# Keeping VectorE's and ScalarE's instructions in source order in a decoder block on one Trainium2 core

## The chip, the core and the metric

The kernel runs on one core of a Trainium2 chip. TensorE (PE) multiplies matrices out of SBUF into banks of PSUM, VectorE (DVE) and ScalarE (ACT) work on tiles elementwise, GpSimd (POOL) does a few small things, and SyncE (SP) issues nearly all DMA transfers. Each engine works through its own list of instructions in order and waits at an instruction until what it needs is done. The metric is the device time of one launch in microseconds (us), as the median of several runs. The kernel before takes 1941.25 us.

## What is computed

One layer of a decoder trunk for 256 tokens of width 2048, all in float32: adaptive norms, two token mixers side by side (retention and a short gated convolution), merged by gates, then a gated feed-forward part with a depthwise convolution.

```python
mod = c_act @ w_ada[l] + b_ada[l]
sh1, sc1, g1, sh2, sc2, g2 = [m[:, None, :] for m in jnp.split(mod, 6, axis=-1)]
xn = _rmsnorm(h, norm1_g[l]) * (1.0 + sc1) + sh1
proj = xn @ w_in[l]
q, k, v, g_ret, bg, cg, xc, gate_logits = jnp.split(proj, splits, axis=-1)
...
y_ret = _retention_chunkwise(q, k, v).reshape(b, s, D_RET)
y_ret = (y_ret * jax.nn.silu(g_ret)) @ w_ret_o[l]
y_conv = bg * _causal_dwconv(cg * xc, w_sc[l])
y_conv = y_conv @ w_conv_o[l]
gates = jax.nn.sigmoid(gate_logits + b_gate[l])
gate_a, gate_b = jnp.split(gates, N_BRANCHES, axis=-1)
mixed = (gate_a * y_ret + gate_b * y_conv) @ w_mix_o[l]
h = h + g1 * mixed
xn2 = _rmsnorm(h, norm2_g[l]) * (1.0 + sc2) + sh2
up = xn2 @ w_up[l]
gt = _causal_dwconv(xn2 @ w_gate[l], w_ffconv[l], b_ffconv[l])
ff = (jax.nn.silu(gt) * up) @ w_down[l]
h = h + g2 * ff
return _rmsnorm(h, final_g)
```

## The kernel before

Nearly all time is matrix products with weights that are read once. A float32 product is made of float32r products: every weight tile is split into a rounded part `hi` (a cast on ACT, line 304) and the rest `lo` (a subtraction on DVE, line 305), and activations are kept split in the same way (`split`, lines 90 to 95).

The program is a list of **units**. A `Weights` unit loads a tile of 256 x 512 weights (`raw`, 512 KB, seven buffers), splits it and multiplies it: 16 matmuls in a block of `w_block` (weights stationary, four accumulators; 8 with `hi`, lines 409, and 8 half as wide with `lo`, line 414), 12 in a block of `x_block` (activations stationary, lines 376 to 378). Eight units make one block over the 2048 rows. When a block ends, ACT copies half of each accumulator (`sb`, line 420) and DVE adds the other half to it. An `Ada` unit loads a tile of `w_ada` into the same `raw` buffers and has no matmul: DVE alone adds it to an accumulator (`ada`, line 341). `spread` puts the `Ada` units between the `Weights` units. `Call` and `Loaded` units do single steps, such as a gate's bias and sigmoid, or a part of the second norm (`normed`).

The blocks follow each other so: a first stage in chunks (to about 390 us); the projections for retention with its rotations, scores and mixing (`rot_block`, `retention`), and three blocks C, X and B of the convolution's group 0; the retention's output projection; the convolution's groups 1 to 3 (`conv_blocks`: at the end of X the product u x cg, four scalings on ACT at line 746, and eight tap operations on DVE); the convolution's output projection, the mixing projection, the second norm (about 1195 us), and the feed-forward part.

The loop that writes the program takes a step per unit: it calls `load` for the unit nine places ahead, `prep` (the `hi` and `lo`, or the `ada`) for the unit two places ahead, `run` (the matmuls and what ends a block), and then the functions that earlier steps left for this one (`after`). That is the order of the source. It isn't the order on the engines: a scheduler orders each engine's instructions by data and buffers, and takes one ahead of another where it expects it to be ready, except where an instruction is told to keep its place (`tc.keep_in_program_order`, used in the first stage for a few).

Of the kernel before, what the change touches and what calls it, by code (L numbers as in the profile page):

```python
# [15 lines left out]
ALU = mybir.AluOpType  # L16
# [30 lines left out]
def tile_trunk_block(  # L47
# [6 lines left out]
    nc = tc.nc  # L54
    x, positions, out = x[0], positions, out[0]
# [34 lines left out]
    def split(src, dst):  # L90

        nc.scalar.copy(dst[:, :, 0, :], src)  # L92
        nc.vector.tensor_tensor(
            dst[:, :, 1, :], src, dst[:, :, 0, :].bitcast(F32), op=ALU.subtract
        )
# [10 lines left out]
    nc.vector.memset(warm, 0.0)  # L106
    nc.scalar.activation(warm, warm, AF.Sigmoid)
# [11 lines left out]
    def turned(vec, n, dst):  # L119
        pt = misc_bank()  # L120
        nc.tensor.transpose(pt[:, :n], vec[:n, :], ident[:n, :n])
        nc.vector.tensor_copy(dst, pt[:, :n])
        return dst
# [3 lines left out]
    nc.scalar.activation(c_act, c_raw, AF.Sigmoid)  # L127
    nc.vector.tensor_mul(c_act, c_act, c_raw)
# [96 lines left out]
    def sumsq(src, acc_col):  # L225
        junk = small.tile([P, 512], BF16, tag="junk", bufs=1, name=nm("junk"))
        n = src.shape[-1]
        return nc.scalar.activation(junk[:, :n], src, AF.Square, accum_out=acc_col)
# [5 lines left out]
    for t in range(2):  # L234
# [3 lines left out]
        nc.vector.tensor_reduce(ss_t, ss_x[:, t], axis=mybir.AxisListType.X, op=ALU.add)  # L238
        r_x = rstd_of(ss_t, 1, D, "r_x")
        nc.vector.tensor_scalar_mul(diag[t], ident, r_x[:, 0:1])  # L240
    x_t = [blk8("x_t", [P, 8, S], F32) for _ in range(2)]
    for g in range(8):
# [8 lines left out]
        nc.scalar.copy(x_t[g // 4][:, 2 * (g % 4):2 * (g % 4) + 2, :].rearrange("p k s -> p (k s)"), pt)  # L251
# [30 lines left out]
    class Weights:  # L282
# [11 lines left out]
        def prep(self):  # L294
# [9 lines left out]
            nc.scalar.copy(self.hi, self.raw)  # L304
            nc.vector.tensor_tensor(self.lo, self.raw, self.hi.bitcast(F32), op=ALU.subtract)  # L305
# [4 lines left out]
    class Ada:  # L310
# [23 lines left out]
        def prep(self):  # L334
            acc = self.state["acc"]
            for k in range(self.nk):
                kt = self.k0 + k
                if kt == 0 and not self.bias:
                    nc.vector.tensor_scalar_mul(acc, self.raw[:, k], c_act[:, 0:1])
                    continue  # L340
                nc.vector.scalar_tensor_tensor(  # L341
# [19 lines left out]
    def shift_of(ps, b, bias, k0, n):  # L361
        nc.vector.tensor_tensor(b[:, k0:k0 + n], ps, bias[:, k0:k0 + n], op=ALU.add)

    def scale_of(ps, a, bias, norm, k0, n):
        sl = slice(k0, k0 + n)
        nc.vector.tensor_tensor(a[:, sl], ps, bias[:, sl], op=ALU.add)
        nc.vector.scalar_tensor_tensor(
# [29 lines left out]
    def w_block(w, c0, xt, epilogue):  # L397
# [3 lines left out]
        def run_at(k0):  # L401
            def run(u):
                if k0 == 0:
                    st["ps"] = [acc_bank() for _ in range(4)]
                for i in range(4):
# [12 lines left out]
                    if last:  # L418
                        b = small.tile([P, S], F32, tag="sb", name=nm("sb"))
                        nc.scalar.copy(b, ps[:, S:2 * S])  # L420
# [14 lines left out]
    def xn1_ready(k0, k1):  # L435
        def done(acc):
# [4 lines left out]
            for k in sorted({k0, *range(k0 + k0 % 2, k1, 2)}):  # L441
                m = 1 if k % 2 else min(2, k1 - k)
                xk = x_t[k // 8][:, k % 8:k % 8 + m, :]
                for i in range(m):
                    kt = k + i
                    nc.scalar.activation(
# [18 lines left out]
    def start_block(j, in_psum):  # L465
# [8 lines left out]
        def finish(t, ps, n):  # L474
            d = dst[t]
            if in_psum or n == 0:
                nc.scalar.copy(d, ps)
            else:
                nc.vector.tensor_tensor(d, ps, d, op=ALU.add)
# [3 lines left out]
        def swish(d):  # L483
            sig = work.tile([P, CB], F32, tag="xtmp", bufs=2, name=nm("sig"))
            nc.scalar.activation(sig, d, AF.Sigmoid)
            nc.vector.tensor_tensor(d, d, sig, op=ALU.mult)
# [51 lines left out]
    def broadcast(acc, store, half, name, bank):  # L538
        if "t" not in store:
            store["t"] = blk8(name, [P, D], F32)  # L540
        for s in range(2):
# [3 lines left out]
            nc.scalar.copy(store["t"][:, c0:c0 + CB], ps)  # L545
# [43 lines left out]
    def rotate(xx, store, key):  # L589
        o = {}  # L590

        def turn(n):
            v = nc.vector.tensor_tensor
# [18 lines left out]
    def rot_block(col, store, key):  # L612
        xs = {}

        def e(i, a, b):
            if i == 0:
                xs["x"] = w4("qk", [P, 4, S])
            nc.vector.tensor_tensor(xs["x"][:, i, :], a, b, op=ALU.add)
# [4 lines left out]
    def retention(pair, st):  # L623

        def scores():
            st["pt"] = []
            pts = w4("pt", [P, 2, S + P])
            for h2 in range(2):
# [9 lines left out]
                nc.vector.tensor_tensor(pt[:, 0:S], ps[:, 0:S], st["dec"][:, h2, :], op=ALU.mult)  # L638
                nc.vector.tensor_tensor(pt[:, S:S + P], ps[:, S:S + P], st["dec"][:, h2, 0:P], op=ALU.mult)
# [3 lines left out]
        def mix():  # L643
# [78 lines left out]
    def conv_blocks(j):  # L722
        st = {}

        def e_c(i, a, b):
            if i == 0:
                st["c"] = w4("cg", [P, 4, S])
            nc.vector.tensor_tensor(st["c"][:, i, :], a, b, op=ALU.add)

        def e_x(i, a, b):  # L730
# [3 lines left out]
            nc.vector.tensor_tensor(st["u"][:, i, 2:S + 2], a, b, op=ALU.add)  # L734
# [5 lines left out]
        def gate_x():  # L740
            u = st["u"][:, :, 2:S + 2]
            st["y"] = w4("conv", [P, 4, S])
            nc.vector.tensor_tensor(u, u, st["c"], op=ALU.mult)
            for i in range(4):
                t = 4 * j + i
                nc.scalar.mul(st["y"][:, i, :], u[:, i, :], wsc[:, 32 + t:33 + t])

        def taps(i0):
            for i in range(i0, i0 + 2):
                u, y, t = st["u"][:, i, :], st["y"][:, i, :], 4 * j + i  # L750
                nc.vector.scalar_tensor_tensor(
                    y, u[:, 1:S + 1], wsc[:, 16 + t:17 + t], y, op0=ALU.mult, op1=ALU.add)
                nc.vector.scalar_tensor_tensor(
                    y, u[:, 0:S], wsc[:, t:t + 1], y, op0=ALU.mult, op1=ALU.add)

        def e_b(i, a, b):
            if i == 0:
                st["b"] = w4("bg", [P, 4, S])
            nc.vector.tensor_tensor(st["b"][:, i, :], a, b, op=ALU.add)
            if i == 3:  # L760
                after(1, lambda: nc.vector.tensor_tensor(st["y"], st["y"], st["b"], op=ALU.mult))
# [44 lines left out]
    def conv_o_block(j):  # L806
        cols = slice(j * CB, (j + 1) * CB)

        def e(t, ps):
            a, b = gate_a[t][:, cols], gate_b[t][:, cols]  # L810
            nc.vector.tensor_tensor(b, ps, b, op=ALU.mult)
            nc.vector.tensor_tensor(a, a, b, op=ALU.add)
# [26 lines left out]
    def residual(j, t, ps, gate):  # L839
        cols = slice(j * CB, (j + 1) * CB)  # L840
        tmp = work.tile([P, CB], F32, tag="xtmp", bufs=2, name=nm("res"))
        nc.vector.tensor_tensor(tmp, ps, gate["t"][:, cols], op=ALU.mult)
        nc.vector.tensor_tensor(h_tok[t][:, cols], h_tok[t][:, cols], tmp, op=ALU.add)
# [3 lines left out]
    def turn_h(j):  # L847
# [3 lines left out]
        for g in range(2):  # L851
# [7 lines left out]
            nc.scalar.copy(h_t[j // 2][:, k0:k0 + 2, :].rearrange("p k s -> p (k s)"), ps)  # L859
# [21 lines left out]
    def norm2():  # L881
        ss = small.tile([P, 2], F32, tag="ss2", name="ss_h2")
        nc.vector.tensor_reduce(ss, ss_h, axis=mybir.AxisListType.X, op=ALU.add)
        r = rstd_of(ss, 2, D, "r_h")
        dr = w4("dr", [P, 2, P])
        for t in range(2):
            nc.vector.tensor_scalar_mul(dr[:, t, :], ident, r[:, t:t + 1])
# [5 lines left out]
    def normed(k0, k1):  # L893
        for kt in range(k0, k1):
# [195 lines left out]
```

## Time and profile before

| | |
|---|---|
| time, median of 3 runs | 1941.25 us (1940.28 to 1943.81) |
| time of the profiled execution | 1944.93 us |
| its span | 1943.1 us |
| PE busy | 1876.3 us, 97% |
| DVE busy | 1380.0 us, 71% |
| ACT busy | 891.1 us, 46% |
| mean bandwidth of DMA | 233 GB/s |

The span is what the profile sees of one execution; 1.83 us of its time lie around it. An engine's busy time counts its instructions, not its waits. PE's clock is granted by the chip and shown as a share of full speed.

### The profile page before, as it was taken

How to read it: one execution, taken by the hardware profiler on the slowest of the kernel's cores; microseconds unless marked ns; L12 is line 12 of the kernel's file. 1: busy time of each engine (PE TensorE's matmuls, PEld its weight loads, DVE VectorE, ACT ScalarE, POOL GpSimd, SP SyncE). 2: the span in 40 equal slices, each digit the busy share in tenths (PEclk: the TensorE clock that was granted, in tenths of full speed). 3: DMA queues.
4: the chain of work that ended last, by engine and by line, in shares of the span. 5: the costliest groups of instructions: out<-in, count | busy, mean ns of one | idle time of the engine just before them, and what ended most of it. 6: DMA issues, size and time to landing. Idle time of an engine off the chain costs nothing.

```text
span 1943.1 us, 25273 instructions
## 1 busy us (share of the span) xinstructions
PE 1876.3 (97%) x9543; PEld 1582.6 (81%) x9543; DVE 1380.0 (71%) x1638; ACT 891.1 (46%) x1150; POOL 21.8 (1%) x51
## 2 busy tenths in 40 slices
PE   5999999999999999999989999999999999999997
PEld 4788888878888877888778777888888888888886
DVE  6899987867688865677677766777765556666655
ACT  4643444534334543444444445555554335555543
POOL 1000000000000000000000000000000000000000
PEclk9999999999999999999999999999999999999999
DMA  8889986667777777787777885777665556666553
GB/s 300 305 278 308 319 306 188 207 220 242 235 234 246 237 250 245 263 269 248 249 241 259 290 266 153 232 230 225 218 205 194 192 192 192 188 192 207 193 193 112
DMA packets 222091, 452.89 MB, mean 233 GB/s; under 512 B 14932, under 2 KB 27536, under 8 KB 221584
## 3 DMA queue, kind: packets, MB, share of 16 engines
q1 hardware_dynamic: 220768, 448.99, 70.3%
q10 hardware_dynamic: 720, 2.10, 0.3%
q8 instruction: 75, 1.23, 0.2%
q14 instruction: 48, 0.39, 0.1%
q0 software_dynamic: 480, 0.18, 0.0%
HBM read 449.11 MB, written 2.10 MB: 232 GB/s over the span
## 4 chain that ended last, share of the span: by engine, by line
PE 81%; DMA 9%; DVE 6%; issue 3%; ACT 1%; SPq 0%; POOL 0%; DVEq 0%; POOLq 0%; ACTq 0%
PE acc L409 30%; PE acc L414 15%; PE acc L377 12%; PE acc L378 12%; PE acc L376 12%; DMA raw<-in_w_ada 7%; DVE lo L305 3%; DVE ada L341 1%; DMA ld<-in_b_gate 1%; PE misc L355 1%; PE misc L247 0%; ACT hi L304 0%; DMA raw<-in_w_mix_o 0%; DMA raw<-in_w_in 0%; DVE y_tok L660 0%
## 5 line engine op out<-in xcount | busy, mean ns | idle before, releaser
L304 ACT CAST hi<-raw 128x1024 fp32r<-128x1024 f32 (+1 forms) x601 | 622.9, 1038 | 837.1 <-PE acc L409 426.5
L305 DVE TENSOR_TENSOR lo<-raw,hi 128x1024 fp32r<-128x1024 f32 (+1 forms) x601 | 717.9, 1203 | 302.4 <-ACT hi L304 299.3
L409 PE MATMUL acc<-xn,hi 128*128 128x512 f32 x2688 | 852.0, 398 | 5.6 <-DVE u L734 2.5
L414 PEld LDWEIGHTS acc<-xn,lo 128*128 128x128 f32 x2688 | 507.1, 189 | 129.6 <-DVE lo L305 9.9
L414 PE MATMUL acc<-xn,lo 128*128 128x256 f32 x2688 | 531.3, 279 | 6.7 <-DVE lo L305 6.7
L409 PEld LDWEIGHTS acc<-xn,hi 128*128 128x128 f32 x2688 | 412.9, 190 | 8.8 <-DVE u L734 2.9
L341 DVE SCALAR_TENSOR_TENSOR ada<-raw,c_act,ada 128x1024 f32<-128x1024 f32 (+2 forms) x199 | 238.9, 1201 | 177.6 <-DMA raw<-in_w_ada 176.9
L377 PE MATMUL acc<-lo,ff_t 128*128 128x512 f32 x332 | 129.2, 389 | 0.0
L376 PE MATMUL acc<-hi,ff_t 128*128 128x512 f32 x332 | 129.2, 389 | 0.0
L378 PE MATMUL acc<-hi,ff_t 128*128 128x512 f32 x332 | 129.2, 389 | 0.0
L376 PE MATMUL acc<-hi,xn 128*128 128x512 f32 x304 | 119.0, 395 | 4.1 <-ACT xn L92 2.4
L377 PE MATMUL acc<-lo,xn 128*128 128x512 f32 x304 | 119.8, 394 | 1.1 <-DVE lo L305 1.1
L378 PE MATMUL acc<-hi,xn 128*128 128x512 f32 x304 | 119.4, 393 | 0.0
L420 ACT COPY sb<-acc 128x256 f32<-128x256 f32 x168 | 61.9, 370 | 44.4 <-PE acc L414 28.4
L378 PE MATMUL acc<-hw,xn 128*128 128x512 f32 x208 | 82.0, 394 | 0.0
L377 PE MATMUL acc<-lw,xn 128*128 128x512 f32 x208 | 81.9, 394 | 0.0
L376 PE MATMUL acc<-hw,xn 128*128 128x512 f32 x208 | 81.1, 394 | 0.0
L304 ACT CAST hw<-raw 128x1024 fp32r<-128x1024 f32 (+1 forms) x58 | 55.6, 959 | 48.4 <-DMA raw<-in_w_in 27.2
L377 PEld LDWEIGHTS acc<-lo,ff_t 128*128 128x128 f32 x332 | 62.3, 188 | 13.2 <-DVE lo L305 0.2
L376 PEld LDWEIGHTS acc<-hi,ff_t 128*128 128x128 f32 x332 | 62.3, 188 | 13.0
L378 PEld LDWEIGHTS acc<-hi,ff_t 128*128 128x128 f32 x332 | 62.3, 188 | 12.7
L376 PEld LDWEIGHTS acc<-hi,xn 128*128 128x128 f32 x304 | 57.1, 188 | 17.7 <-ACT xn L92 2.4
(195 smaller groups left out, 1762.4 us busy)
## 6 DMA issues: line engine op xcount, KB each, us to landing
raw<-in_w_in SPq DMA_DIRECT2D x272, 512.0 KB, 4.7
raw<-in_w_ada SPq DMA_DIRECT2D x160, 512.0 KB, 4.6
raw<-in_w_gate SPq DMA_DIRECT2D x88, 512.0 KB, 4.1
raw<-in_w_up SPq DMA_DIRECT2D x88, 512.0 KB, 4.1
raw<-in_w_down SPq DMA_DIRECT2D x88, 512.0 KB, 4.3
raw<-in_w_ret_o SPq DMA_DIRECT2D x32, 512.0 KB, 5.2
raw<-in_w_conv_o SPq DMA_DIRECT2D x32, 512.0 KB, 5.0
raw<-in_w_mix_o SPq DMA_DIRECT2D x32, 512.0 KB, 6.1
```

The source lines that it names most:

```text
L304: nc.scalar.copy(self.hi, self.raw)
L305: nc.vector.tensor_tensor(self.lo, self.raw, self.hi.bitcast(F32), op=ALU.subtract)
L341: nc.vector.scalar_tensor_tensor(acc, self.raw[:, k], c_act[:, kt:kt + 1], acc, op0=ALU.mult, op1=ALU.add)
L355: nc.tensor.matmul(ps[:, i:i + 1], lhsT=flat[:, (s0 + i) * P:(s0 + i + 1) * P], rhs=ones[:, 0:1], start=True, stop=True,)
L376: nc.tensor.matmul(ps, lhsT=xh, rhs=u.hi[:, k, :], start=k0 + k == first, stop=False)
L377: nc.tensor.matmul(ps, lhsT=xh, rhs=u.lo[:, k, :], start=False, stop=False)
L378: nc.tensor.matmul(ps, lhsT=xl, rhs=u.hi[:, k, :], start=False, stop=k0 + k == end - 1)
L409: nc.tensor.matmul(ps, lhsT=u.hi[:, k, i * P:(i + 1) * P], rhs=xt(k0 + k).rearrange("p h s -> p (h s)"), start=k0 + k == 0, stop=False,)
L414: nc.tensor.matmul(ps[:, 0:S], lhsT=u.lo[:, k, i * P:(i + 1) * P], rhs=xt(k0 + k)[:, 0, :], start=False, stop=last and k == UK - 1,)
L420: nc.scalar.copy(b, ps[:, S:2 * S])
```

## The change

A small class stands in front of `nc.vector` and `nc.scalar`. Once `ordered[0]` is set, each instruction that is issued through it is told to keep its place in the order of the source among the instructions told so on its engine. It is set in the main loop from the unit `n_start` on, twelve units before the end of the first stage. All instructions of DVE and ACT from there on are ordered so; those of PE, SP and POOL stay with the scheduler. No instruction, tile or buffer is added or taken away.

```diff
+    ordered = [False]
+
+    class Ordered:
...
+        def __init__(self, engine):
+            self.engine = engine
+
+        def __getattr__(self, name):
+            fn = getattr(self.engine, name)
+
+            def issue(*args, **kw):
+                ins = fn(*args, **kw)
+                return tc.keep_in_program_order(ins) if ordered[0] else ins
+            return issue
+
+    vector, scalar = Ordered(nc.vector), Ordered(nc.scalar)
...
-            nc.scalar.copy(self.hi, self.raw)
-            nc.vector.tensor_tensor(self.lo, self.raw, self.hi.bitcast(F32), op=ALU.subtract)
+            scalar.copy(self.hi, self.raw)
+            vector.tensor_tensor(self.lo, self.raw, self.hi.bitcast(F32), op=ALU.subtract)
...
         now[0] = i
+        ordered[0] = i >= n_start
         units[i].run()
```

All other lines of the diff put `vector` and `scalar` where `nc.vector` and `nc.scalar` stood. In the lists below, line 67 is the line of `ins = fn(...)` in the new class, and stands for all of them.

DVE at the end of block X of the convolution's group 2, before (901 to 912 us). `u` is the accumulator's sum, `lo_` and `ada_` are as above, a `raw_` with a lower number was loaded earlier, and `conv_` are the taps:

```order
L305 TENSOR_TENSOR lo_7588<-raw_7469,hi_7587 128x1024
L341 SCALAR_TENSOR_TENSOR ada_7066<-raw_7591,c_act,ada_7066 128x1024
L734 TENSOR_TENSOR u_7600<-acc_7427,sb_7598 128x256
L734 TENSOR_TENSOR u_7600<-acc_7428,sb_7607 128x256
L305 TENSOR_TENSOR lo_7627<-raw_7497,hi_7626 128x1024
L734 TENSOR_TENSOR u_7600<-acc_7429,sb_7614 128x256
L305 TENSOR_TENSOR lo_7659<-raw_7516,hi_7658 128x1024
L734 TENSOR_TENSOR u_7600<-acc_7430,sb_7621 128x256
L743 TENSOR_TENSOR u_7600<-u_7600,cg_7395 128x4x256
L305 TENSOR_TENSOR lo_7692<-raw_7544,hi_7691 128x1024
L751 SCALAR_TENSOR_TENSOR conv_7650<-u_7600,vec_t,conv_7650 128x256 x2
L753 SCALAR_TENSOR_TENSOR conv_7650<-u_7600,vec_t,conv_7650 128x256 x2
```

The same place of DVE in the changed program:

```order
L67 TENSOR_TENSOR u_7600<-acc_7430,sb_7621 128x256
L67 TENSOR_TENSOR lo_7627<-raw_7497,hi_7626 128x1024
L67 TENSOR_TENSOR u_7600<-u_7600,cg_7395 128x4x256
L67 TENSOR_TENSOR lo_7659<-raw_7516,hi_7658 128x1024
L67 SCALAR_TENSOR_TENSOR conv_7650<-u_7600,vec_t,conv_7650 128x256 x4
L67 SCALAR_TENSOR_TENSOR ada_7066<-raw_7538,c_act,ada_7066 128x1024
L67 SCALAR_TENSOR_TENSOR conv_7650<-u_7600,vec_t,conv_7650 128x256 x4
L67 TENSOR_TENSOR lo_7692<-raw_7544,hi_7691 128x1024
L67 TENSOR_TENSOR lo_7714<-raw_7563,hi_7713 128x1024
L67 TENSOR_TENSOR lo_7720<-raw_7585,hi_7719 128x1024
L67 SCALAR_TENSOR_TENSOR ada_7066<-raw_7591,c_act,ada_7066 128x1024
```

The `ada` of raw_7591 moved from before the four adds to behind lo_7720, and lo_7659 and lo_7692 moved from before the product and the taps to behind them.

ACT at the same place of the changed program, where `hi_` are the casts, and the four `conv_` scalings stand between two of them:

```order
L67 COPY sb_7621<-acc_7430 128x256
L67 CAST hi_7626<-raw_7497 128x1024
L67 ACTIVATE conv_7650<-u_7600,vec_t 128x256 x4
L67 CAST hi_7658<-raw_7516 128x1024
L67 CAST hi_7691<-raw_7544 128x1024
```

Before, hi_7658 and hi_7691 stood ahead of the scalings; they moved behind them.

DVE where the feed-forward part begins, before. `dr` is the reciprocal root of the norm on a diagonal, `u` the normed column block, `xn` its `lo` part (its `hi` part is made of `u` on ACT):

```order
L887 TENSOR_SCALAR dr_9925<-ident,r_h_9922 128x128 x2
L899 SCALAR_TENSOR_TENSOR u_9952<-h_t_9435,a_219,acc_9947 128x256
L899 SCALAR_TENSOR_TENSOR u_9956<-h_t_9435,a_219,acc_9947 128x256
L899 SCALAR_TENSOR_TENSOR u_9960<-h_t_9435,a_219,acc_9947 128x256
L902 SCALAR_TENSOR_TENSOR xn_1968_9951<-u_9952,b_220,xn_1968_9951 128x256
L902 SCALAR_TENSOR_TENSOR xn_1968_9951<-u_9956,b_220,xn_1968_9951 128x256
```

The same in the changed program, somewhat further down in it, where two units follow each other:

```order
L67 SCALAR_TENSOR_TENSOR xn_1968_9951<-u_9964,b_220,xn_1968_9951 128x256
L67 TENSOR_TENSOR lo_9969<-raw_9828,hi_9968 128x1024
L67 SCALAR_TENSOR_TENSOR u_9995<-h_t_9435,a_219,acc_9947 128x256
L67 SCALAR_TENSOR_TENSOR xn_1980_9994<-u_9995,b_220,xn_1980_9994 128x256
L67 SCALAR_TENSOR_TENSOR u_9999<-h_t_9435,a_219,acc_9947 128x256
L67 SCALAR_TENSOR_TENSOR xn_1980_9994<-u_9999,b_220,xn_1980_9994 128x256
L67 TENSOR_TENSOR lo_10004<-raw_9862,hi_10003 128x1024
```

Groups of three `u` and three `xn` became single ones in turn, with a `lo` behind each two.

## Rows read from the trace of the kernel before

**Rows 1.** The page: TensorE's busy time, and the chain that ended last by engine.

```profile
PE 1876.3 (97%) x9543; PEld 1582.6 (81%) x9543; DVE 1380.0 (71%) x1638; ACT 891.1 (46%) x1150; POOL 21.8 (1%) x51
PE 81%; DMA 9%; DVE 6%; issue 3%; ACT 1%; SPq 0%; POOL 0%; DVEq 0%; POOLq 0%; ACTq 0%
```

**Rows 2.** Windows: stretch, length, busy us of each engine, granted clock, DMA share, GB/s.

```profile
390.00:700.00 310.00, 299.50 (x1668) 258.83 (x1667) 237.40 (x290) 134.62 (x198) 4.11 (x5) 0.98 0.73 237
700.00:1200.00 500.00, 476.94 (x2373) 396.45 (x2372) 341.48 (x364) 210.72 (x257) 7.09 (x14) 0.99 0.76 252
1204.00:1922.00 718.00, 718.00 (x3814) 615.43 (x3813) 466.17 (x538) 355.52 (x439) 0.96 (x9) 1.00 0.62 199
1250.00:1300.00 50.00, 50.00 (x289) 43.64 (x288) 36.85 (x42) 26.34 (x33) 0.21 (x2) 1.00 0.73 231
425.00:429.00 4.00, 3.73 (x13) 3.01 (x12) 3.97 (x7) 1.14 (x2) 0.00 (x0) 0.57 0.93 325
1012.00:1016.00 4.00, 4.00 (x13) 3.11 (x12) 2.28 (x3) 1.01 (x1) 0.00 (x0) 0.58 0.84 258
```

**Rows 3.** Waits, 390 to 1200 us: who waits for whom, us, times, longest us.

```profile
DVE ada L341 <- DMA raw<-in_w_ada: 166.3, 80, 5.4
...
DVE lo L305 <- ACT hi L304: 41.7, 43, 2.4
...
PE acc L377 <- DVE lo L305: 12.5, 10, 2.1
...
PE acc L414 <- DVE lo L305: 6.7, 7, 1.7
```

**Rows 4.** Timeline of DVE, end of block X: start, us, line, tiles, [idle before <-releaser].

```profile
901.83 1.28 DVE L341 SCALAR_TENSOR_TENSOR ada<-raw,c_act,ada 128x1024 f32<-128x1024 f32 x1 [4.60 <-DMA raw<-in_w_ada]
903.03 0.75 DVE L734 TENSOR_TENSOR u<-acc,sb 128x256 f32<-128x256 f32 x2
...
906.75 1.23 DVE L743 TENSOR_TENSOR u<-u,cg 128x1024 f32<-128x1024 f32 x1
907.89 1.22 DVE L305 TENSOR_TENSOR lo<-raw,hi 128x1024 fp32r<-128x1024 f32 x1
909.03 0.87 DVE L751 SCALAR_TENSOR_TENSOR conv<-u,vec_t,conv 128x256 f32<-128x256 f32 x2
```

**Rows 5.** Timeline of PE at the same place.

```profile
903.50 0.73 PE L409 MATMUL acc<-xn,hi 128*128 128x512 f32 x2 [1.42 <-DVE u L734]
```

**Rows 6.** Timeline of ACT at the same place.

```profile
903.54 0.37 ACT L420 COPY sb<-acc 128x256 f32<-128x256 f32 x1 [1.99 <-DVE u L734]
...
908.07 1.71 ACT L746 ACTIVATE conv<-u,vec_t 128x256 f32<-128x256 f32 x4 [2.05 <-DVE u L743]
```

**Rows 7.** Timeline of DVE, start of the feed-forward part.

```profile
1197.65 1.26 DVE L899 SCALAR_TENSOR_TENSOR u<-h_t,a,acc 128x256 f32<-128x256 f32 x3 [1.06 <-PE acc L891]
...
1200.02 1.25 DVE L899 SCALAR_TENSOR_TENSOR u<-h_t,a,acc 128x256 f32<-128x256 f32 x3
...
1216.50 1.23 DVE L305 TENSOR_TENSOR lo<-raw,hi 128x1024 fp32r<-128x1024 f32 x1 [0.38 <-ACT hi L304]
1217.64 0.48 DVE L902 SCALAR_TENSOR_TENSOR xn<-u,b,xn 128x256 fp32r<-128x256 f32 x1
1218.04 0.47 DVE L899 SCALAR_TENSOR_TENSOR u<-h_t,a,acc 128x256 f32<-128x256 f32 x1
```

**Rows 8.** Timeline of ACT, start of the feed-forward part.

```profile
1215.42 1.05 ACT L304 CAST hi<-raw 128x1024 fp32r<-128x1024 f32 x1 [0.93 <-ACT xn L901]
1216.37 0.50 ACT L901 ACTIVATE xn<-u,b 128x256 fp32r<-128x256 f32 x1
...
1224.23 0.35 ACT L420 COPY sb<-acc 128x256 f32<-128x256 f32 x1
```

**Rows 9.** Timeline of PE, start of the feed-forward part.

```profile
1196.65 0.96 PE L891 MATMUL acc<-dr,ones 128*128 128x256 f32 x2 [2.10 <-DVE dr L887]
1199.36 1.65 PE L409 MATMUL acc<-xn,hi 128*128 128x512 f32 x3 [1.75 <-DVE xn L902]
```

More of the change, by code (lines that the diff above doesn't have):

```diff
@@ L90, in split @@
     def split(src, dst):
-        nc.scalar.copy(dst[:, :, 0, :], src)
-        nc.vector.tensor_tensor(
+        scalar.copy(dst[:, :, 0, :], src)
+        vector.tensor_tensor(
             dst[:, :, 1, :], src, dst[:, :, 0, :].bitcast(F32), op=ALU.subtract
@@ L250, in tile_trunk_block @@
                 )
-        nc.scalar.copy(x_t[g // 4][:, 2 * (g % 4):2 * (g % 4) + 2, :].rearrange("p k s -> p (k s)"), pt)
+        scalar.copy(x_t[g // 4][:, 2 * (g % 4):2 * (g % 4) + 2, :].rearrange("p k s -> p (k s)"), pt)
     a1 = const.tile([P, KT], F32, name="a1")
@@ L419, in run @@
                         b = small.tile([P, S], F32, tag="sb", name=nm("sb"))
-                        nc.scalar.copy(b, ps[:, S:2 * S])
+                        scalar.copy(b, ps[:, S:2 * S])
                         epilogue(i, ps[:, 0:S], b)
@@ L476, in finish @@
             if in_psum or n == 0:
-                nc.scalar.copy(d, ps)
+                scalar.copy(d, ps)
             else:
-                nc.vector.tensor_tensor(d, ps, d, op=ALU.add)
+                vector.tensor_tensor(d, ps, d, op=ALU.add)
             if n == len(chunks) - 1 and q == 1:
@@ L544, in broadcast @@
             c0 = (2 * half + s) * CB
-            nc.scalar.copy(store["t"][:, c0:c0 + CB], ps)
+            scalar.copy(store["t"][:, c0:c0 + CB], ps)
     def gate1_done(half):
@@ L592, in turn @@
         def turn(n):
-            v = nc.vector.tensor_tensor
+            v = vector.tensor_tensor
             if n == 0:
@@ L841, in residual @@
         tmp = work.tile([P, CB], F32, tag="xtmp", bufs=2, name=nm("res"))
-        nc.vector.tensor_tensor(tmp, ps, gate["t"][:, cols], op=ALU.mult)
-        nc.vector.tensor_tensor(h_tok[t][:, cols], h_tok[t][:, cols], tmp, op=ALU.add)
+        vector.tensor_tensor(tmp, ps, gate["t"][:, cols], op=ALU.mult)
+        vector.tensor_tensor(h_tok[t][:, cols], h_tok[t][:, cols], tmp, op=ALU.add)
     h_t = []
@@ L858, in turn_h @@
             k0 = 4 * (j % 2) + 2 * g
-            nc.scalar.copy(h_t[j // 2][:, k0:k0 + 2, :].rearrange("p k s -> p (k s)"), ps)
+            scalar.copy(h_t[j // 2][:, k0:k0 + 2, :].rearrange("p k s -> p (k s)"), ps)
     def mix_epilogue(j):
@@ L923, in e_g @@
                 after(3, sigmoid)
-                after(4, lambda: nc.vector.tensor_tensor(st["y"], st["y"], st["s"], op=ALU.mult))
+                after(4, lambda: vector.tensor_tensor(st["y"], st["y"], st["s"], op=ALU.mult))
         def taps(i0):
```

108 lines of the change are left out of this document (54 added, 54 removed).

## The prediction

> **What bounds the kernel now.** I read the engine shares first. TensorE (PE) is busy 97% of the span and the chain that ended last is 81% PE, but 9% of it is DMA and 6% VectorE (DVE) [rows 1]: PE is the bound except in short stops. The windows say where the stops are. From 390 to 700 us PE is busy 299.50 of 310, from 700 to 1200 us 476.94 of 500, from 1204 to 1922 us 718.00 of 718 [rows 2]. So in the part whose order changes there are 10.5 + 23.1 = 33.6 us of idle PE, all before 1204 us, and none after. Where PE idles its clock falls too: from 425 to 429 us, just behind a stop, the granted clock is 0.57 in the mean [rows 2], which is mostly the lower of its two levels (1.2 of 2.4 GHz); one such dip loses 4 x (1 - 0.57) = 1.7 us. The mean clock of 0.98 over 390 to 700 us [rows 2] is what three dips give (5.1 of 310), and one more stands at 1012 us [rows 2]: four before 1195 us.
>
> Then who waits for whom between 390 and 1200 us [rows 3]. DVE stands 166.3 us, in 80 waits, in front of an `ada` operation (line 341) for the load of its `w_ada` tile. PE waits directly for `lo` (line 305) 12.5 + 6.7 us. The instructions show how the two hang together [rows 4]: an `ada` starts at 901.83 us after 4.60 us of idle DVE, and behind it stand the adds that empty the accumulators (`u`) and `lo`. PE, which needs one of those banks back, stands 1.42 us until 903.50 [rows 5]. DVE had nothing to do for 4.60 us, and the work that PE waited for was ready and stood one place further back.
>
> **What the change does to that, and the gain.** In the order of the changed program `ada` stands in the order of the loads: the `ada` that waited at 901.83 (raw_7591) moves from a place before lo_7627 to a place behind lo_7720. Tiles are then used in the order in which they were asked for, nine units ahead. A unit keeps PE 16 matmuls; at 289 in 50 us [rows 2] that is 2.77 us. So the load has several units' time to land and the 166.3 us of waits should be nearly gone. If all stops go, PE gains the 33.6 us less the 3.85 us at the start of the feed-forward part, which are no `ada` waits (2.10 for `dr`, 1.75 for `xn` [rows 9]): 29.8. The four clock dips give back 4 x 1.7 = 6.8. Together -36.6 us. This is the upper end of the gain, since a few stops (the retention chain) have another cause.
>
> **What source order costs, one place in full: the end of convolution block X of group 2.** Before, DVE runs lo_7627 and lo_7659 between the four `u` adds, and lo_7692 before the taps; the preparation of three units is through before the long gating work. After, lo_7659 stands behind u x cg, and its `hi` on ScalarE (ACT) behind the four conv scalings; lo_7692 stands behind all taps. With T = PE's last matmul of the block, all in us:
> - ACT copies the last `sb` (0.37), then `hi` of unit 2 (1.05 [rows 8]) to T+1.4; `lo` of unit 2 1.22 to T+2.7.
> - DVE u x cg 1.23 to T+3.8; ACT four scalings 1.71 [rows 6] to T+5.6, `hi` of unit 3 to T+6.7.
> - PE has unit 1 prepared, works units 1 and 2 to T+5.54, then waits for that `hi`: 1.2.
> - DVE: `lo` of unit 3 to T+8.0, four taps (two take 0.87 [rows 4], 0.40 each from start to start), the `ada` (1.20 from start to start [rows 4]), four taps, `lo` of unit 4 at T+13.5. PE has finished unit 3 at T+9.5, and runs unit 4's `hi` half for about 1.8: it waits 2.2 more.
>
> So 3.3 us, where before lost 1.42. Walked in the same way, with the same durations: the four X ends together 7.9; retention (block ends with an `ada` or a decay unit in the lookahead of two, and the step where the cast of `y_t` stands ahead of the next `hi`) 9.5; the two passages from a B block to a projection, where gate adds, sigmoids and the cast of `conv_t` stand ahead of `hi`, 8.6; the output and mix blocks 5.6. Together 31.6. The ends: half of it (16), if the units that are prepared hide more than I gave them, and 40, if each walk misses one hand-over. I keep 31.6 since the walk above uses rows at each step. New stops cost clock as well: two dips, 3.4.
>
> **The start of the feed-forward part.** Here before writes three `u`, then three `xn`, so that ACT works on one while DVE works on the next. After, `u` and `xn` alternate strictly, and each `xn` on DVE needs ACT's result of the `u` just before. One column block is then u 0.47 + ACT 0.50 + xn 0.40 (start to start, 1217.64 to 1218.04 in rows 7) + two hand-overs of 0.03 (ACT's `hi` ends at 1216.47, `lo` starts at 1216.50) = 1.43 us [rows 7, 8]; before does three in 2.37 (1197.65 to 1200.02), 0.79 each. A unit needs two blocks, then `hi` 1.05 (behind the second ACT `xn`), then `lo` 1.14 to the next start. DVE's cycle for a unit is 1.43 + 0.47 + 0.03 + 0.50 + 1.05 + 0.03 + 1.14 = 4.65 us against PE's 2.77. From the first `u`: four blocks 5.7, the second unit's `hi` and `lo` to 7.6, then a cycle of 4.65 for each of the other six; the third unit's `hi` is ready at 11.1, the last one's at 11.1 + 5 x 4.65 = 34.4 and PE ends at 37.1. Before, the same block of eight units takes from 1197.65 to 1223.9 (its last `sb` copy starts at 1224.23 [rows 8]), 26.2. That is +10.9. Ahead of it a `hi` and a `lo` now stand between the last residual and the reduction that norm2 begins with: +1.4. PE would be 60% busy here and lose clock once more than now, +1.7. Sum: +14.0; without clock 12.3, and 17 if the clock stays low through most of it.
>
> From 1224 us on nothing is idle and I find no new stop: a unit's DVE work there (`lo` 1.14, four taps 1.6) fits in 2.77, and two prepared units cover the block ends. Cost 0; if that cover fails at each of 21 block ends by 0.3 us, +6. The tail keeps its order except for the last tiles' `hi` and `lo`, whose 1.14 a unit is under the 1.36 of a half unit on PE: 0.
>
> **Sum.** -36.6 + 31.6 + 3.4 + 14.0 = +12.4 us. On the profiled run's 1944.93 us (its span 1943.1 plus 1.83 around it) that is 1957.3. The profiled run lies 3.7 above the median of the three runs, so the median would be 1941.25 + 12.4 = 1953.7.
>
> **Rivals.**
> *A, faster.* The `ada` waits go and the new stops are mostly hidden: DVE is busy only 341 of 500 us [rows 2], so once it waits for nothing it may stand well ahead of PE when a block ends. Half the new stops (16), no new dips, feed-forward start +10.9: -36.6 + 16 + 10.9 = -9.7, 1931.5; if that start also costs only half, 1926. For it: the gain rests on measured waits, the loss on a walk. Against it: lookahead is two places however free DVE is, and `ada`, decay and gate units use up places. It decides when a block end costs under about 1.5 us on average.
> *B, the loads are the bound.* DVE's waits for `w_ada` stay, because too few load buffers make each load start late, and source order adds its own stops. Then I take off only half of the gain: -18 + 31.6 + 3.4 + 14.0 = +31, 1972. Against it: DMA is busy 0.73 to 0.76 in the stretch [rows 2], and the wait is at tiles taken ahead of older ones. The Trainium skill, page "Perfetto Trace Analysis", section Optimization Strategy, reads repeated gaps of one kind on the engine that should be saturated as a possible sign that too few tiles can be allocated; by that rule the stops would stay where they are. No run here has another number of buffers, so the trace only speaks by the places above.
> *C, no change.* Gain and loss cancel, about 1941: new stops of 19 instead of 31.6. Or the change does little on the chip: the orders differ at all the places named, so I give that no more than 2 in 100.
>
> **How the numbers follow.** My sum (slower, 1947 to 1966) 0.50, B 0.08, A 0.31, C 0.11. Slower by over 0.2% 0.58, within 0.2% 0.11, faster by over 0.2% 0.31; 0.2%, 3.9 us, is about what a measurement of this kernel can tell from no change. The predicted time is the sum's, 1954 us; its own range is 1947 to 1966. For 8 in 10 the range has to take in most of A and the lower part of B: 1927 to 1971.
>
> **What would show it.** Right: DVE's waits for `w_ada` under 20 us; DVE waits for ACT's `hi` longer than the 41.7 of now [rows 3]; PE stops behind X ends and at the passages to the projections; `u` and `xn` alternating with the first gate block over 35 us long; PE full from about 1235 us. Wrong: `w_ada` waits that stay (B); idle PE between 390 and 1195 us under 20 us (A); a first gate block under 30 us; new idle PE after 1240 us, which I have at nothing.

## The result, and the profile after

The changed kernel takes 1964.61 us (median of 4 runs, 1964.24 to 1965.79) against 1941.16 us (1940.28 to 1943.81): 1.0128 of the time before, 95% interval 1.0104 to 1.0151. It is slower, as forecast, and inside the range (1927 to 1971), but by 23.5 us where the sum said 12.4. On the profiled executions, against which the sum was made, it is 1965.79 against 1944.93, 20.9 us; the profiled run of before was 3.8 us above its median, that of the changed kernel 1.2.

The page of the changed kernel (engine, busy us, share, instructions; then two groups of instructions with busy us, mean ns, idle before and its cause):

```profile
PE 1886.3 (96%) x9543; PEld 1586.4 (81%) x9543; DVE 1397.6 (71%) x1638; ACT 885.0 (45%) x1150; POOL 21.8 (1%) x51
...
L67 ACT CAST hi<-raw 128x1024 fp32r<-128x1024 f32 (+1 forms) x601 | 616.1, 1036 | 681.7 <-PE acc L395 322.9
...
L67 DVE SCALAR_TENSOR_TENSOR ada<-raw,c_act,ada 128x1024 f32<-128x1024 f32 (+2 forms) x199 | 238.7, 1200 | 0.4
```

The idle time in front of `ada` fell to 0.4 us in the whole program; between 390 and 1200 us it had been 166.3 [rows 3]. So the change does what it is for. PE's busy time rose by 10 us with the same matmuls. A part is clock, since a matmul at half clock is shown as busy for longer: PE is busy for 22.0 us at the lower clock in the trace of before and for 29.0 us in this one, which is some 3.5 us more of busy time for the same work. The rest isn't traced to a cause. Windows of the changed kernel (stretch, length, busy us of PE, PEld, DVE, ACT, POOL, granted clock, DMA share, GB/s):

```profile
390.00:700.00 310.00, 297.49 (x1662) 255.87 (x1661) 232.54 (x278) 124.78 (x184) 4.10 (x5) 0.99 0.71 234
700.00:1200.00 500.00, 482.32 (x2376) 400.45 (x2374) 353.12 (x366) 211.38 (x263) 6.21 (x11) 0.99 0.75 254
1203.00:1240.00 37.00, 27.45 (x127) 22.16 (x128) 23.82 (x41) 16.19 (x26) 0.10 (x1) 0.91 0.36 113
1240.00:1930.00 690.00, 688.68 (x3653) 589.05 (x3652) 447.30 (x506) 333.75 (x413) 0.95 (x9) 1.00 0.64 203
692.00:700.00 8.00, 5.71 (x13) 4.09 (x14) 6.80 (x6) 2.60 (x4) 0.00 (x0) 0.57 0.58 178
914.00:918.00 4.00, 4.00 (x18) 3.47 (x18) 3.92 (x4) 0.44 (x1) 0.00 (x0) 0.60 0.86 271
1005.00:1014.00 9.00, 6.62 (x16) 4.94 (x17) 6.66 (x7) 3.35 (x4) 0.00 (x0) 0.62 0.63 184
1060.00:1066.00 6.00, 5.47 (x17) 4.03 (x16) 4.36 (x4) 2.40 (x3) 0.00 (x0) 0.72 0.62 151
```

Beside [rows 2]: PE is idle nearly as much (12.5 + 17.7 us, against 10.5 + 23.1), but elsewhere. Without the stops at the second norm, which fall into the window of before with 3.9 us and into that of after with 0.3, it is 29.9 us against 29.7. The dips of its clock at 692 and 1005 us are worth 3.4 us each (8 x 0.43, 9 x 0.38), twice one of before. New is the stretch 1203 to 1240 us with 9.6 us of idle PE. Who waits between 390 and 1200 us:

```profile
DVE lo L67 <- ACT hi L67: 124.9, 121, 3.6
...
PE acc L426 <- ACT hi L67: 8.6, 8, 1.7
...
PE acc L431 <- DVE lo L67: 8.2, 6, 2.4
...
PE acc L394 <- DVE lo L67: 6.9, 8, 1.9
...
PE acc L393 <- ACT hi L67: 5.8, 3, 2.1
```

DVE's wait for ACT's `hi` went from 41.7 to 124.9 us, and PE now waits for `hi` itself (14.4 us), which it didn't before.

**The walk at block X, on the chip.** The end of block X of group 2 on DVE, then ACT, then PE (start, us, engine, line, tiles, idle before). PE works two prepared units (5.54 us) before its first stop at 905.14, so its last matmul of the block is at about 899.6 us, which is T:

```profile
902.10 1.22 DVE L67 TENSOR_TENSOR u<-u,cg 128x1024 f32<-128x1024 f32 x1
906.09 1.23 DVE L67 TENSOR_TENSOR lo<-raw,hi 128x1024 fp32r<-128x1024 f32 x1 [2.77 <-ACT hi L67]
907.23 1.92 DVE L67 SCALAR_TENSOR_TENSOR conv<-u,vec_t,conv 128x256 f32<-128x256 f32 x4
909.07 1.28 DVE L67 SCALAR_TENSOR_TENSOR ada<-raw,c_act,ada 128x1024 f32<-128x1024 f32 x1
910.26 1.92 DVE L67 SCALAR_TENSOR_TENSOR conv<-u,vec_t,conv 128x256 f32<-128x256 f32 x4
912.09 3.49 DVE L67 TENSOR_TENSOR lo<-raw,hi 128x1024 fp32r<-128x1024 f32 x3
```

```profile
903.41 1.71 ACT L67 ACTIVATE conv<-u,vec_t 128x256 f32<-128x256 f32 x4 [2.48 <-DVE u L67]
905.03 2.93 ACT L67 CAST hi<-raw 128x1024 fp32r<-128x1024 f32 x3
```

```profile
906.11 1.67 PE L426 MATMUL acc<-xn,hi 128*128 128x512 f32 x6 [0.97 <-ACT hi L67]
...
913.37 1.21 PE L431 MATMUL acc<-xn,lo 128*128 128x256 f32 x8 [2.35 <-DVE lo L67]
```

The cast behind the four scalings ends at T+6.5, and PE stops 0.97 us for it; the `lo` behind all taps and the `ada` is done at T+13.7, and PE stops 2.35. Together 3.32 us; the walk said 3.3, where before lost 1.42 [rows 5].

**The start of the feed-forward part.** ACT, then DVE, one cycle, and PE's stops:

```profile
1216.52 0.51 ACT L67 ACTIVATE xn<-u,b 128x256 fp32r<-128x256 f32 x1 [1.68 <-DVE u L67]
1217.98 0.51 ACT L67 ACTIVATE xn<-u,b 128x256 fp32r<-128x256 f32 x1 [0.94 <-DVE u L67]
1218.39 1.03 ACT L67 CAST hi<-raw 128x1024 fp32r<-128x1024 f32 x1
```

```profile
1214.87 1.23 DVE L67 TENSOR_TENSOR lo<-raw,hi 128x1024 fp32r<-128x1024 f32 x1 [0.45 <-ACT hi L67]
1216.01 0.47 DVE L67 SCALAR_TENSOR_TENSOR u<-h_t,a,acc 128x256 f32<-128x256 f32 x1
1217.07 0.48 DVE L67 SCALAR_TENSOR_TENSOR xn<-u,b,xn 128x256 fp32r<-128x256 f32 x1 [0.58 <-ACT xn L67]
1217.47 0.47 DVE L67 SCALAR_TENSOR_TENSOR u<-h_t,a,acc 128x256 f32<-128x256 f32 x1
1218.52 0.48 DVE L67 SCALAR_TENSOR_TENSOR xn<-u,b,xn 128x256 fp32r<-128x256 f32 x1 [0.57 <-ACT xn L67]
1219.45 1.23 DVE L67 TENSOR_TENSOR lo<-raw,hi 128x1024 fp32r<-128x1024 f32 x1 [0.45 <-ACT hi L67]
```

```profile
1203.20 0.70 PE L908 MATMUL acc<-dr,ones 128*128 128x256 f32 x2 [3.52 <-DVE dr L67]
...
1219.47 1.67 PE L426 MATMUL acc<-xn,hi 128*128 128x512 f32 x6 [1.50 <-ACT hi L67]
1224.05 1.65 PE L426 MATMUL acc<-xn,hi 128*128 128x512 f32 x6 [1.50 <-ACT hi L67]
```

DVE's cycle, from `lo` to `lo`, is 4.58 us (1214.87 to 1219.45); the sum had 4.65. The wait for `dr` is 3.52 where it was 2.10 [rows 9]: the `hi` and `lo` ahead of the reduction cost 1.4, as forecast.

**Where the 20.9 us are.** PE's start of the same step in both traces, as the difference after minus before: +0.6 at 399 us, before the changed order has an effect on PE (it is as much at 210 us); -3.2 at the retention's output projection (688.23 and 685.03); +8.1 at the mixing projection (1096.33 and 1104.44); +6.5 at the row matmul of the second norm (1196.65 and 1203.20); +17.2 at the first down block (1470.73 and 1487.90), and the same +17.2 at the second (1824.22 and 1841.41); +20.8 at the last matmul.

### The profile page after: what moved, and what is told of

Read it like the earlier page. It is cut to its first block, busy times and chain, and to the rows that moved or that the text cites. A ratio compares the mean times of both kernels' runs of the same rounds, so it can differ in the third digit from the quotient of the medians.

```text
span 1964.0 us, 25281 instructions
## 1 busy us (share of the span) xinstructions
PE 1886.3 (96%) x9543; PEld 1586.4 (81%) x9543; DVE 1397.6 (71%) x1638; ACT 885.0 (45%) x1150; POOL 21.8 (1%) x51
## 5 line engine op out<-in xcount | busy, mean ns | idle before, releaser
L67 ACT CAST hi<-raw 128x1024 fp32r<-128x1024 f32 (+1 forms) x601 | 616.1, 1036 | 681.7 <-PE acc L395 322.9
L426 PE MATMUL acc<-xn,hi 128*128 128x512 f32 x2688 | 838.5, 398 | 17.9 <-ACT hi L67 15.3
L431 PEld LDWEIGHTS acc<-xn,lo 128*128 128x128 f32 x2688 | 495.0, 189 | 123.8 <-DVE lo L67 13.6
L431 PE MATMUL acc<-xn,lo 128*128 128x256 f32 x2688 | 520.1, 280 | 8.2 <-DVE lo L67 8.2
L426 PEld LDWEIGHTS acc<-xn,hi 128*128 128x128 f32 x2688 | 419.7, 190 | 30.4 <-ACT hi L67 17.9
L393 PEld LDWEIGHTS acc<-hi,xn 128*128 128x128 f32 x304 | 57.5, 190 | 17.7 <-ACT xn L67 2.4
```

What stands on the lines that cost most here:

```text
L67: ins = fn(*args, **kw)
L393: nc.tensor.matmul(ps, lhsT=xh, rhs=u.hi[:, k, :], start=k0 + k == first, stop=False)
L426: nc.tensor.matmul(ps, lhsT=u.hi[:, k, i * P:(i + 1) * P], rhs=xt(k0 + k).rearrange("p h s -> p (h s)"), start=k0 + k == 0, stop=False,)
L431: nc.tensor.matmul(ps[:, 0:S], lhsT=u.lo[:, k, i * P:(i + 1) * P], rhs=xt(k0 + k)[:, 0, :], start=False, stop=last and k == UK - 1,)
```

## The experiments

The kernel before took 1941 us on the chip of the result, and 1929 to 1942 us from run to run on the three of the experiments (e1 to e4, e5 to e8, e9 to e11). No trace of it was taken there; the one of [rows 1] to [rows 9] is of an execution of 1944.93 us, longer than any of these. Ratios are to the runs of before beside them. Unless said otherwise the edit is to the changed kernel.

**e1: `u` and `xn` free.** In `normed`:

```diff
-            vector.scalar_tensor_tensor(
+            nc.vector.scalar_tensor_tensor(
...
-            scalar.activation(xk[:, 0, :], u, AF.Identity, bias=b2[:, kt:kt + 1])
+            nc.scalar.activation(xk[:, 0, :], u, AF.Identity, bias=b2[:, kt:kt + 1])
...
```

> The changed kernel, but the u and xn instructions of the second norm's parts (normed) are left to the scheduler again, so that three u and three xn stand in groups as before. Theory: the alternation costs the start of the feed-forward part 10.6 us (PE is 6.55 us behind the kernel before at the row matmul, 17.2 us behind after the first gate and up blocks), so the time falls from 1964.6 to about 1954 and the first gate block takes about 26 us from the first u. Rival: the hi and lo of the weights, two units ahead, are what binds there; then u and xn in groups change little and the time stays above 1960.

1955.81 us, ratio 1.0122 (1.0107 to 1.0137); 8.8 us less than the changed kernel's 1964.61, and 10.6 less than in e5, on other chips. The traces say it without a change of chip: from the row matmul to the first down block PE takes 284.7 us in the changed kernel (1203.20 to 1487.90), 275.0 in e1 (1202.87 to 1477.88), and 274.1 before (1196.65 to 1470.73). The first gate block takes 25.7 us from the first `u` (1203.61) to its first `sb` copy (1229.35), 35.4 in the changed kernel (1203.93 to 1239.35) and 24.3 before. The alternation of `u` and `xn` is what this start costs, but for about 1 us.

**e2: source order only up to the second norm.**

```diff
+    n_norm2 = len(units)
     units.append(Call(norm2))
...
-        ordered[0] = i >= n_start
+        ordered[0] = n_start <= i < n_norm2 - PREP_AHEAD
```

> The order of the source only from the last twelve units of the first stage to the second norm; from there on the scheduler is free. Theory: the part up to the norm costs 5 to 8 us by itself (PE 8.1 us behind at the start of the mixing projection, 6.55 at the row matmul), and nothing else: 1941.2 + 5 to 8 = 1946 to 1949. Rival: the stretch before the norm brings a gain by itself, as the waits for w_ada are gone, and all loss is in the feed-forward part: below 1938.

1949.20 us, ratio 1.0089 (1.0072 to 1.0106). The rival that has all the loss in the feed-forward part is out: the part before the norm is by itself slower than the free order. The 1946 to 1949 were met only because they were counted from the time of before on the chip of the result: beside its own runs of before (1933.66) e2 is 15.5 us slower, not 5 to 8. Against the changed kernel's 1964.61 it is 15.4 us faster, as the traces have it for what lies behind its end: 1.4 + 10.6 + 3.6 = 15.6.

**e3 and e11: one engine alone.**

```diff
-    vector, scalar = Ordered(nc.vector), Ordered(nc.scalar)
+    vector, scalar = Ordered(nc.vector), nc.scalar
```

and for e11 the other way round.

> Only VectorE is held to the order of the source, ScalarE is left to the scheduler. Theory: PE's stops on hi (about 21 us of the 43.8 us of idle PE after 390 us) come from casts that stand behind block-end work on ScalarE; with them free most of these stops and some of the clock dips go, 1964.6 - 20 = 1945 (1938 to 1950). Rival: the casts are late because VectorE's chain ahead of them is late (they wait for it); then the time stays within 5 us of 1964.6.

> Only ScalarE is held to the order of the source, VectorE is left to the scheduler, the lookahead is as in the kernel before. Theory: ada still stands ahead of older tiles on VectorE, and hi stands behind block-end work on ScalarE: slower than before, but with neither the whole of the one loss nor of the other: 1938 + 5 to 15 = 1943 to 1953. Rival: ScalarE's order alone makes the whole loss (above 1960), or none (within 4 us of before).

e3: 1949.66 us, 1.0091 (1.0076 to 1.0106); e11: 1952.21 us, 1.0078 (1.0054 to 1.0103), beside other runs of before. Both are within what was expected. With VectorE alone in order, PE waits for no `hi` any more, but 21.3 us for `lo` (15.1 in the changed kernel, 390 to 1200 us). With ScalarE alone, DVE still waits 129.8 us for `w_ada`, and PE 9.4 us for `hi`. Each engine's order brings a part of the loss.

**e4: only `lo` and `ada` in order.** The kernel before, with `tc.keep_in_program_order` around these alone, from the same unit on.

> The kernel before, with only the lo and ada instructions of VectorE kept in source order among each other (from the same unit on); all block-end work is free. Theory: this alone takes away the 166 us of VectorE's waits for w_ada and the stops behind them, and adds few new stops: 1941.2 - 15 to - 28, so 1913 to 1926. Rival: the stops come from a lookahead of two units that a block end uses up, whoever stands first; then the gain is under 8 us, 1933 to 1945.

1937.08 us, 1.0012 (0.9996 to 1.0028). My theory fell here, and the rival held. DVE waits for no `w_ada` any more, and yet nothing is gained beside its runs of before. Waits of this kernel, 390 to 1200 us:

```profile
PE acc L419 <- DVE lo L310: 9.8, 12, 1.5
PE acc L382 <- DVE lo L310: 9.3, 5, 2.7
```

PE waits for `lo` as long as before (19.1 us, against 19.2 in [rows 3]). All its idle time before the norm is some 22 us, less than the 29.7 in the trace of before, but no less than in e7 below, where the order is free and `w_ada` is waited for (some 22 as well). So the stops weren't only those of a wrong order: at a block's end there were too few prepared units. That the scheduler's hoisting of weights past the block-end work had been hiding part of that fits, but isn't shown by itself.

**e6 and e7: another lookahead, with and without the order.** The loop prepares the unit two places ahead, whatever it is, so an `Ada`, decay or gate unit uses up a place. Now a unit is prepared as soon as fewer than three weight units are prepared and not yet run (three is what the buffers of `hi` and `lo` hold). e6 is e1 with this, e7 the kernel before with this.

```diff
-        while prepped <= min(i + ahead, n - 1):
+        while prepped < n:
+            if prepped > i + ahead:
+                live = sum(isinstance(u, Weights) for u in units[max(i, 0):prepped])
+                if i < n_start or prepped > i + 7 or isinstance(units[prepped], Weights) and live >= 3:
+                    break
             units[prepped].prep()
             prepped += 1
```

> The changed kernel with u and xn of the second norm free, as in e1, and with another rule for the lookahead: the next unit is prepared as soon as fewer than three weight units are prepared and not yet run, so that ada, decay and gate units no longer use up places. Theory: the stops before the norm come from block-end work that finds only one or two weight units prepared; with three they mostly go, and with them the clock dips: e1's 1955.8 less about 22 us of stops and 8 us of clock, 1926 (1920 to 1935). Rival: VectorE's and ScalarE's chains at block ends (about 13 us in the walk at block X) are longer than any lookahead that three buffers allow; then the time stays above 1945.

> The kernel before, with nothing held in order, and the lookahead rule of e6 alone. Theory: the scheduler already takes preparations ahead of block-end work, so the rule brings it little, and ada stays ahead of older tiles: within 6 us of the kernel before. Rival: the rule alone is what matters, and this kernel is as fast as e6 or faster (under 1926).

e6: 1913.18 us, ratio 0.9882 (0.9860 to 0.9903), faster than both kernels and by more than I expected. e7: 1936.09 us, 0.9997 (0.9980 to 1.0014): the rule alone brings nothing. Windows and waits of e6 (390 to 1155 us, where its norm begins):

```profile
390.00:690.00 300.00, 299.12 (x1691) 259.61 (x1690) 235.30 (x280) 128.00 (x186) 4.11 (x5) 1.00 0.75 246
690.00:1095.00 405.00, 404.39 (x2070) 340.43 (x2070) 308.58 (x326) 183.43 (x226) 6.22 (x11) 1.00 0.82 274
1095.00:1155.00 60.00, 59.99 (x271) 49.25 (x270) 40.11 (x39) 26.46 (x33) 0.00 (x0) 1.00 0.78 259
```

```profile
DVE lo L67 <- ACT hi L67: 143.7, 142, 3.7
PE acc L431 <- DVE lo L67: 0.8, 2, 0.6
PE acc L426 <- DVE qk L67: 0.6, 1, 0.6
```

Before the norm 1.5 us of idle PE are left, at full clock. DVE waits for ACT's `hi` longer than ever (143.7 us), and PE waits for `lo` for 0.8 us in all, as units stand ready. And a wait of e7, 390 to 1200 us:

```profile
DVE ada L341 <- DMA raw<-in_w_ada: 160.9, 80, 5.7
```

With the scheduler free, `ada` stands ahead of older tiles whatever the lookahead. The two causes hide each other: order alone leaves the short lookahead (e1, e4), lookahead alone leaves DVE in front of the loads (e7), and both together take away nearly all stops. No run joins the lookahead with e4's order of `lo` and `ada` alone, so it isn't shown how much of e6's gain is the place of `ada` and how much the place of the other instructions.

**e5: the changed kernel again**, with no edit, beside e6 to e8.

> The changed kernel itself once more, beside the other runs of this call, since the kernel before took 1941 us on the chip of the first result and 1934 us on that of the experiments so far. Theory: the changed kernel waits for no transfer, so its time is the same on every chip: 1964 to 1966, with a spread under 2 us. Rival: it differs between chips as the kernel before does: 1955 to 1960.

1966.39 us (1962.24 to 1967.07), ratio 1.0155 (1.0130 to 1.0179), while 13 runs of before lie between 1929.2 and 1941.0. It is not as constant as I had expected (one run of four lies 4 us under the others), but it doesn't follow the kernel before to shorter times: the order that waits for no load has about the time of the first result, and the free order differs by 12 us from run to run. That its stops hang on when a load lands would fit, but isn't shown; e4, which waits for no `w_ada`, differs by 5.5 us.

**e8: is it the clock?** 16 matmuls on the weights just used, into an accumulator that nothing reads, behind the second unit of the two projections' first blocks; the products of these blocks are kept in order around them.

```diff
...
+                if fill and k0 == UK:
+                    extra = acc_bank()
+                    for n in range(fill):
+                        tc.keep_in_program_order(nc.tensor.matmul(
+                            extra, lhsT=xt(k0)[:, 0, 0:P], rhs=u.hi[:, 0, :],
+                            start=n == 0, stop=n == fill - 1))
...
```

> The changed kernel with 16 more matmuls (3.6 us at full clock, on an accumulator that nothing reads) between the second and the third unit of the retention's and of the convolution's output projection, where TensorE stands 3.6 and 4.0 us and the clock is at half for 3.4 us of loss each time behind it. Theory: the stop costs its own length and as much again by the clock; with TensorE kept busy the stop's length stays, the loss of clock goes: 1964.6 - 5 to - 7. Rival: the clock falls for another reason or the added work costs its own time: 1964.6 or up to 7 us more.

1960.32 us (1958.60 to 1965.10), 6.1 less than e5 beside it; one of its four runs lies among those of e5. The two stretches, first in e5, then in e8:

```profile
692.00:700.00 8.00, 5.20 (x12) 3.74 (x13) 7.02 (x6) 2.90 (x4) 0.00 (x0) 0.59 0.53 167
1005.00:1013.00 8.00, 5.12 (x12) 3.77 (x13) 7.02 (x6) 2.82 (x3) 0.00 (x0) 0.66 0.50 154
```

```profile
692.00:700.00 8.00, 7.13 (x32) 5.56 (x31) 7.49 (x7) 3.92 (x4) 0.00 (x0) 1.00 0.58 176
1004.00:1012.00 8.00, 7.13 (x32) 5.55 (x31) 7.11 (x7) 2.83 (x3) 0.00 (x0) 1.00 0.63 190
```

With more work to do the kernel is faster: the clock stays at full speed in both places. But not all of the 6.1 us come from there. The start of the same DVE instruction in both traces, e8 minus e5, goes from -0.2 to -2.1 us at the first place and from -2.1 to -4.6 at the second, so filling brought 1.9 and 2.4 us. The rest lies at other dips, each worth 1.6 us, in stretches that the edit doesn't touch: e5 has one at 914 and one at 1060 us that e8 hasn't, and e8 one at 840 us that e5 hasn't. In that order:

```profile
914.00:920.00 6.00, 6.00 (x29) 5.29 (x30) 4.42 (x4) 1.72 (x2) 0.00 (x0) 0.72 0.81 274
1060.00:1066.00 6.00, 5.22 (x15) 3.84 (x16) 4.78 (x5) 2.40 (x4) 0.00 (x0) 0.72 0.48 141
838.00:844.00 6.00, 4.84 (x21) 4.31 (x22) 6.00 (x6) 1.05 (x1) 0.00 (x0) 0.72 0.82 273
```

So a stop is paid twice here, by its length (3.6 and 4.0 us) and by 1.9 and 2.4 us of clock behind it; the theory's "as much again" is too much, and part of the 6.1 is luck. PE's order is held around the extra matmuls as well; no run holds it without them.

**e9 and e10: what is left.** e9 is the changed kernel with e6's lookahead and nothing else; e10 is e6 with the second norm's start and the ends of the last four down blocks free as well (`ordered[0] = False` while they are issued).

> The changed kernel, everything in source order as it is, with e6's lookahead rule (three weight units prepared and not yet run). Theory: the rule takes away the stops before the norm, but the alternation of u and xn at the start of the feed-forward part is in the source and stays: e6's 1913.2 + 8 to 11 = 1921 to 1924. Rival: a third prepared unit hides the alternation as well, and the time is within 3 us of e6's.

> e6 with the second norm's start and the ends of the last three down blocks also left to the scheduler, as in the kernel before. Theory: the reduction comes ahead of the next hi and lo again (1.4 to 1.6 us less idle before the row matmul), the three stops of 0.53 us go and the tail is as in the kernel before: 1913.2 - 3 to - 5 = 1908 to 1910. Rival: these stops are given back by the scheduler's other choices; within 1 us of e6.

e9: 1923.11 us, ratio 0.9937 (0.9915 to 0.9958), 9.9 more than e6: three prepared units don't hide the alternation of `u` and `xn`. e10: 1906.09 us (1904.46 to 1909.74), 0.9847 (0.9825 to 0.9869), the fastest version, 7 us under e6 where I had expected 3 to 5. In its trace the three stops at the ends are gone, the wait for `dr` is 1.75 us where e6 has 3.71, and the dip of the clock behind it is half as long (worth 1.7 us, against 3.4), which the expectation left out.

## Why the prediction was right, and by how much it missed

**The gain.** DVE's 166.3 us of waits for `w_ada` went, all of them, as the first step has it. Rival B, that they come of too few load buffers, is refuted: with the same seven buffers they are gone in the changed kernel and stay at 160.9 us in e7, where the order is free. Nor are the buffers behind PE's stops: with the same ones e6 has 1.5 us of idle PE before the norm. The Trainium skill's page "Perfetto Trace Analysis", section Optimization Strategy, says of repeated gaps on the engine that should be saturated that they can mean too little room for the next tile; the 1.5 us of e6 show that this wasn't the reason here. What didn't come out is a gain from the end of these waits alone: e4 takes them away and gains nothing, so the 36.6 us weren't `ada`'s alone.

**The new stops.** In the changed kernel they add up to 29.9 us before the second norm where I had 31.6, and come one by one at the places walked: X ends 3.3 and 3.3 for groups 1 and 2, the passages into the projections 3.6 and 4.0 (walked 4.3 each), the retention 7.9 (walked 9.5). This step was right. In the sum it only balances the gain, and the sign comes from the feed-forward start; in the runs the stretch before the norm is slower by itself as well (e2, 1.0089).

**The feed-forward start.** From the row matmul to the first down block it cost 10.6 us, and 1.4 ahead of it, 12.0 where I had 14.0. The dip in clock there is as long in both kernels (a mean of 0.57 over 1196 to 1204 us before, of 0.62 over 1203 to 1212 us after, 3.4 us each), so the 1.7 for clock was too much.

**The step that was mis-sized: the clock.** "New stops cost clock as well: two dips, 3.4." Before the norm the dips of before are worth 6.8 us, as I had it; those of after 10.1: at 692 and 1005 us 3.4 each (8 x 0.43, 9 x 0.38), at 914 and 1060 us 1.6 and 1.7 (4 x 0.40, 6 x 0.28). That is more than they cost, since PE also stands idle in the first two (busy 5.71 of 8 and 6.62 of 9 us). Measured by e8 against e5 they cost 1.9, 2.4, 1.6 and 1.6, together 7.5 us, over twice the 3.4. I had two dips of the length that I had seen; there are four, and two are longer. Which stop brings a dip isn't settled by the order: the X ends of groups 1 and 2 stop PE alike (0.97 and 2.4 us), and in e5 only that of group 2 is followed by a dip, in e8 only that of group 1.

By stretch, with PE's starts from above: up to the row matmul the sum had -0.2 (-36.6 + 31.6 + 3.4 + 1.4), and it is +6.0 (0.56 to 6.55); for the feed-forward start +12.6, and it is 10.6; behind it 0, and it is 3.6. Of the 6.2 us missed ahead of the norm the clock is 4.1, and the new stops take off 1.7; 3.8 us stay open. That the total missed by no more than 8.5 us owes something to luck, as the feed-forward start was 2.0 too high.

**The step that failed: the tail.** "0" for what lies behind 1240 us; it is 3.6. Three down blocks end with a stop, such as

```profile
1932.49 0.50 PE L394 MATMUL acc<-hl,ff_t 128*128 128x512 f32 x1 [0.53 <-DVE hl L67]
```

and together they set PE back by 3.6 us (+17.2 to +20.8 above). Here the residual, the final gain and the squares stand ahead of the next `hi` and `lo`. The prediction has two prepared units cover the block ends, and new idle PE after 1240 us stands among its own signs of being wrong. e10, which frees these ends, has no such stop.

**Rivals.** A (faster, since the new stops are hidden) failed by one of its two tests: PE is idle 29.9 us before the norm, where A needed under 20. The other test, a block end under 1.5 us on average, was badly set, as 32 block ends share these 29.9 us, 0.9 each, and the sum's own 31.6 would have met it too. C (no change) is out, as the interval begins at 1.0104. What I had not seen is that the same lookahead limits the kernel before: I took nearly all its stops as due to `ada`, and e4 shows that they don't go with it.

e6 came out 7 us under the range that I gave it. From e1 to e6 42.6 us went. Idle PE before the norm fell from 30.2 to 1.5 us, and e1's dips there, worth 8.5 us, are gone: 37.2 of them; I had taken 22 and 8. The other 5.4 fit with stops that cost more than they show (below), but that wasn't tested by itself. A version with more load buffers wasn't tried.

## What to carry to other kernels

Holding engines to the order of the source takes from the scheduler its bad choices (here an operation on a tile just asked for, ahead of older ones) together with its good ones (weights prepared past block-end work, one engine's step interleaved with another's). Before it is done, count the lookahead in units of the bound engine's work, so that small steps don't use it up, and write chains that go back and forth between two engines in an order that interleaves them; here order and lookahead together, with such a chain left free, gave 0.988 of the time (e6), where order alone gave 1.012 (e1) and lookahead alone 1.000 (e7). An idle time in front of an instruction names what it waited for, not what its removal is worth: 166 us of it went here and the kernel became slower, and in e4, where it went with less else changed, nothing was gained.

## What I had not expected of the hardware

A stop of PE costs more than its idle time in the profile. At the ends of the three down blocks above some 0.66 us of idle are shown each time, and each sets PE back by 1.2 us (3.6 in all): a matmul of 512 columns is shown as busy for 0.39 us, while the next starts 0.23 us after it, so the first part of each stop hides inside the last matmul's record. The first of these ends, with its two stops:

```profile
1873.86 0.39 PE L395 MATMUL acc<-hi,ff_t 128*128 128x512 f32 x1
1874.38 0.73 PE L393 MATMUL acc<-hi,ff_t 128*128 128x512 f32 x2
1875.64 0.50 PE L394 MATMUL acc<-lo,ff_t 128*128 128x512 f32 x1 [0.53 <-DVE lo L67]
1875.98 0.40 PE L395 MATMUL acc<-hi,ff_t 128*128 128x512 f32 x1
```

Each of the two hides 0.16 us so, and the matmul behind each stop takes 0.34 us to the next start, 0.11 more than usual: 0.66 + 0.32 + 0.22 = 1.2.

And adding 32 matmuls to a program made it 6 us faster, 4.3 of them at the two places where they stand and the granted clock stayed at the higher of its two levels. The same stops of some 2.4 us were followed by a dip of the clock in one execution and not in another.
